# One 512-column matmul for the high and low activations of 256-token stages

## The chip, the core and the metric

The kernel runs on one core of one Trainium2 chip. A core has five engines that run side by side, each with its own in-order instruction queue: TensorE (PE in the profile; its weight loads are shown apart as PEld), VectorE (DVE), ScalarE (ACT), GpSimd (POOL) and SyncE (SP), which here issues DMAs. TensorE multiplies a loaded block of weights (128 x 128) with columns that stream past it and adds the products up in PSUM, which has 8 banks of 512 fp32 values in each of 128 partitions. VectorE and ScalarE read PSUM; everything else lies in SBUF. The metric is the device time of one execution in microseconds.

## The reference, cut to what matters

Three transformer layers run over 256 tokens of width 1024: one hybrid layer (a gated delta rule and a linear recurrent unit, then an MLP), a norm, and two layers of a second kind, before which 16 meta tokens are put in front. All of it is fp32.

```python
# block 1
x = x + mix @ w_out
m = rmsnorm(x, norm_mlp_w)
u = relu(m @ w_ff1)                   # 1024 -> 4096
x = x + (u * u) @ w_ff2
x = rmsnorm(x, final_norm_w)
# block 2: 16 meta tokens in front, then twice
h = h + 0.5 * swiglu(rmsnorm(h), gate, up, down)      # silu(x @ gate) * (x @ up) @ down, 1024 -> 2816
q, k, v, a, b, g_sb, g_conv = split(rmsnorm(h) @ w_in)
y_sb = stick_breaking_attention(q, k, v) @ w_attn_out
y_conv = silu(layernorm(conv31(a * sigmoid(b)))) @ w_conv_out
h = h + (sigmoid(g_sb) * y_sb + sigmoid(g_conv) * y_conv) @ w_out
h = h + 0.5 * swiglu(rmsnorm(h), gate, up, down)
return rmsnorm(h)[:, 16:]
```

## The kernel before

**Layout.** Activations lie transposed: channels in the partitions, tokens in the columns. A stage multiplies weights W, 128 x 128 at a time, with the tokens as the moving columns. A stage has 272 columns while the meta tokens are still needed and 256 where they are not: all of block 1, and of layer 1 of block 2 the queries, both gates, both branch outputs, the output projection and the last swiglu.

**Three products for one.** To come near fp32, every operand is held as a high and a low part in the type fp32r (`h`, `lo` for weights; `x.hi`, `x.lo` for activations, made by `split` and `split_scaled`). One k step, that is 128 input channels for one tile of 128 output channels, is three matmuls into the same bank: high weights by high activations (L532), high weights by low activations (L533), low weights by high activations (L534). Each one has its own weight load.

**The stream of weights.** `plan` lists all tiles of weights in the order of use. The kinds that matter here: `ff1`, `ff2` (block 1's MLP), `gate`, `up`, `down` (swiglu), `q`, `gc`, `gs`, `ys`, `yc`, `o2` (mixer of block 2). A unit is up to 8 k steps of one tile (up to 1024 columns). SyncE brings chunks of two units from HBM into `raw`; ScalarE copies a unit to its high part `wh` (`emit_high`); VectorE, or GpSimd for the units listed in `POOLED`, subtracts to get the low part `wl` (`emit_split`). There are 5 buffers of `wh`, 4 of `wl`, and splits run up to three units (`LEAD`) ahead of TensorE.

**Order by hand.** The program writes the order of every queue when it is built. `job` issues the k steps of one tile and calls `tick` after each. All other work is written as flows (Python generators); a table `clk` holds the expected time of each engine, every helper (`act`, `tt`, `ts`, `stt`, `cp`) moves it by an assumed cost, and `tick` lets a flow go on once its inputs are expected to be there, then lays out weight splits while VectorE's clock is not past TensorE's. A flow that is not told to yield lays its operations directly behind each other. The conv taps of the mixer have the state "F": they fill VectorE where it is free.

**Reading the banks.** After a job a flow reads its bank and gives it back (`give`): `do_ff1` (relu on VectorE, square on ScalarE, split into `hid`), `do_ff2`, `evac` in `swiglu` (scale the gate by `R`, silu on ScalarE, product with the up bank, split into `hid`), `residual` (add to `H`, the input and square sums of the next norm), and in the mixer `keep` (q, v), `rows_mul` (k, a, b and the gates), `do_ys` and `do_yc` (products with the sigmoid gates).

**Places of the activations.** `XS` holds the high parts of all k tiles in one tile and the low parts in another, so the two parts of one k tile lie far apart. The core of a k step is

```python
xh, xl = x.hi(k, o, n), x.lo(k, o, n)
nc.tensor.matmul(acc, h[:, s], xh, start=first and done == 0, stop=False)
nc.tensor.matmul(acc, h[:, s], xl, start=False, stop=False)
nc.tensor.matmul(acc, lo[:, s], xh, start=False, stop=last and done == total - 1)
```

Of the kernel before, what the change touches and what calls it, by code (L numbers as in the profile page):

```python
# [16 lines left out]
T1 = 256  # L17
T2 = T1 + NM
KD = 8
# [16 lines left out]
LIMIT0 = 5.0  # L36
ORDER1 = [(c, t) for c in "kqxgvz" for t in range(4)]

# [68 lines left out]
def layout():  # L107
    """units: (job, k tiles, chunk, first column in the chunk); chunks: (offset, columns)."""
# [37 lines left out]
class Arena:  # L146
    """Scratch of the phases: ranges of one tile, by first fit."""
# [61 lines left out]
class Flow:  # L209
    """A chain of operations that is laid out between the others; t: when its last one is expected to end."""  # L210
# [11 lines left out]
def tile_hybrid_blocks(  # L222
# [173 lines left out]
    def force(cond):  # L396
        """Lays out flows, the earliest first, until cond() holds."""
# [108 lines left out]
    def job(kind, x, n, o=0, bank_=None, last=True, start=None):  # L506
        """The products of one tile of output channels over tokens o to o + n, added to those in a bank, if one
        is given; returns the bank."""
# [8 lines left out]
        acc = bank_[:, 0:n]  # L517
        mine = job_units[j]
        total = sum(len(units[u][1]) for u in mine)
        done = 0  # L520
        for u in mine:
# [4 lines left out]
            for i, k in enumerate(units[u][1]):  # L526
# [5 lines left out]
                nc.tensor.matmul(acc, h[:, s], xh, start=first and done == 0, stop=False)  # L532
                nc.tensor.matmul(acc, h[:, s], xl, start=False, stop=False)  # L533
# [7 lines left out]
    def pair(kinds, x, n, o=0):  # L541
        """Two tiles of output channels side by side, the last k tiles after all others."""
# [20 lines left out]
    def rsqrt(s, n):  # L563
        """s (128 x n, in SBUF, overwritten) to s ** -0.5."""
# [23 lines left out]
    def tok_sums(acc, n):  # L588
        """Sums over the channels, one token per partition, a column per block of tokens."""
# [7 lines left out]
    def to_rows(r, n, out=None):  # L597
        """Columns r, one token per partition, as a row in every partition."""
# [9 lines left out]
    def norm_rows(acc, n, inv, eps, out, src, ev, r=None):  # L608
        """out = rsqrt(inv * sum over the channels + eps) in every partition, once src has come."""
# [14 lines left out]
    def root_norm(accs, n, r):  # L624
        """r = (sum over the channels / 1024 + 1e-6) ** -0.5, one token per partition."""
# [13 lines left out]
    class XS:  # L639
        """A stream input: high and low parts of k tiles of n tokens, in one of the two fixed places or in a pool."""  # L640

        def __init__(self, n, k=KD, pool=None, name=None, place=None, o=0):
            if pool is not None:
                self.place = None
                both = [pool.tile([128, k, n], F32R, name=f"{name}{i}") for i in range(2)]
            else:
                self.place = place or places.pop(0)
                both = [p[:, 0:k * n].rearrange("p (a b) -> p a b", a=k) for p in self.place]
            self.h, self.l = both
# [8 lines left out]

        def done(self):
            if self.place:  # L660
                places.append(self.place)

    places = [
        tuple(const.tile([128, KD * T2], F32R, name=f"x{i}{j}") for j in range(2)) for i in range(2)
    ]
# [21 lines left out]
    # =================== block 1: mixer ===================  # L687
# [58 lines left out]
    def room(*dims):  # L746
        """A block of scratch, once there is one."""
# [195 lines left out]
    def sums(i):  # L943
        """rsqrt of the sums of squares of k (0) or q (1), a column per chunk and head."""
# [44 lines left out]
    def sides(c):  # L989
        """What the recurrence over a chunk takes besides the inverse."""  # L990
# [40 lines left out]
    def chunk(c):  # L1031
        """One chunk of 128 tokens, all heads, up to its output."""
# [42 lines left out]
        # the inverse of the unit triangle, blocks doubling from 2 to 128  # L1075
# [195 lines left out]
    # =================== block 1: output projection, MLP ===================  # L1271
    xb = XS(T1, place=xa.place)
    places.remove(xa.place)
    ev_sq2, ev_r2 = Event(), Event()

    def residual(b, m, x, g, sums, ev, o=0, scale=None, add=tt, free=True, bank=None):
        """H += scale * b; the next norm's input and its sums of squares."""
        hm = H[:, m, o:T2]
        if scale is None:
            tt(hm, hm, b[:, 0:T2 - o], ADD)  # L1280
        else:
            t = yield from slot()
            tt(t[:, 0:T2 - o], b[:, 0:T2 - o], scale, MUL)
# [39 lines left out]
    def do_ff1(b, m):  # L1323
        us = yield from slot()
        u = us[:, 0:T1]
        ts(u, b[:, 0:T1], 0.0, ALU.max)
        give(b)
        act(u, u, AF.Square)
# [26 lines left out]
    def do_ff2(b, m):  # L1355
        t = yield from slot()
        tt(t[:, 0:T1], b[:, 0:T1], R2[:, 0:T1], MUL)
        give(b)
        tt(X(m), X(m), t[:, 0:T1], ADD)
# [46 lines left out]
    # =================== block 2 ===================  # L1406
# [432 lines left out]
```

## Time and profile before

| | us |
|---|---|
| median of 3 runs | 1558.58 |
| lowest and highest run | 1553.17, 1559.71 |
| span of the profiled execution | 1560.1 |
| mean granted TensorE clock of that execution | 0.988 |

| stage (from the span's start, by the chain and the timeline) | us |
|---|---|
| block 1: mixer and output projection | 0 to 182 |
| block 1: ff1 and ff2 (256 columns) | 182 to 366 |
| block 2, layer 0 (272 columns) | 366 to 972 |
| layer 1: first swiglu (272 columns) | 972 to 1171 |
| layer 1: mixer (272 and 256 columns) | 1171 to 1363 |
| layer 1: last swiglu (256 columns) | 1363 to 1550 |
| last norm and output | 1550 to 1560 |

The page names an instruction by its line, engine, operation and tiles (written one, arrow, read ones). Nearly all VectorE and ScalarE work carries the line of a helper (L284 for `tt`, L295 for `stt`, L272 for `act`), so groups are told apart by their tiles. Durations of matmuls are modelled and overlap, each lasting longer than the distance to the next, so what a matmul costs is read from the distance of starts, or from a stretch of time divided by its count of matmuls. A VectorE operation of 256 columns is likewise shown with 0.42 us while the next one may start 0.34 us after it.

### The profile page before, as it was taken

The numbers are of one execution on the slowest core, as the hardware profiler recorded it, in microseconds if no ns is written. First come the engines' busy times: TensorE is split into PE (matmuls) and PEld (weight loads), VectorE is DVE, ScalarE is ACT, GpSimd is POOL, SyncE is SP. The second block draws the span as 40 slices with busy tenths as digits, with TensorE's granted clock in tenths as the row PEclk, the third lists the DMA queues.
The fourth block names the chain that finished last, engine by engine and source line by source line (L and its number), as shares of the span: only waits on it lengthen the run. The fifth ranks groups of instructions, "written<-read, shape, count | busy, mean of one in ns | idle before, by whom it ended". The sixth has DMA issues, their size and how long they took to land.

```text
span 1560.1 us, 29338 instructions
## 1 busy us (share of the span) xinstructions
PE 1528.2 (98%) x12160; PEld 1488.3 (95%) x12160; DVE 1065.3 (68%) x1884; ACT 800.1 (51%) x1351; POOL 164.4 (11%) x146
## 2 busy tenths in 40 slices
PE   7999999999999999999999999999999999999997
PEld 7898999999999999889999999999999989999997
DVE  5887866667555578877765555655558976866654
ACT  4568666544444444545544444444444555555443
POOL 3230300000000011114400000000001113500000
PEclk8999999999999999999999999999999999999999
DMA  6312555554545543323555454554554423555552
GB/s 227 136 55 82 184 187 183 183 184 164 188 163 176 176 162 135 136 86 131 175 178 188 155 174 157 191 187 160 172 183 160 162 84 109 175 204 190 183 174 76
DMA packets 36373, 248.75 MB, mean 159 GB/s; under 512 B 3984, under 2 KB 5264, under 8 KB 12304
## 3 DMA queue, kind: packets, MB, share of 16 engines
q1 hardware_dynamic: 35248, 245.63, 44.5%
q8 instruction: 95, 1.56, 0.4%
q10 hardware_dynamic: 992, 1.26, 0.2%
q14 instruction: 38, 0.31, 0.1%
HBM read 245.82 MB, written 1.05 MB: 158 GB/s over the span
## 4 chain that ended last, share of the span: by engine, by line
PE 90%; DVE 6%; ACT 2%; issue 1%; POOL 0%; DMA 0%; POOLq 0%; DVEq 0%; SPq 0%; ACTq 0%
PE bank L532 28%; PE bank L534 27%; PE bank L533 27%; PE bank L315 6%; DVE arena L295 2%; DVE arena L284 1%; PE bank L319 1%; DVE wl L284 1%; ACT arena L272 1%; DVE H L284 1%; ACT wh L272 1%; DVE x L284 0%; DMA H<-in_xt_dram 0%; POOL acc L307 0%; DVE co L284 0%
## 5 line engine op out<-in xcount | busy, mean ns | idle before, releaser
L532 PE MATMUL bank<-x,wh 128*128 128x272 f32 (+1 forms) x2624 | 766.9, 292 | 11.5 <-ACT x L272 10.6
L534 PE MATMUL bank<-x,wl 128*128 128x272 f32 (+1 forms) x2624 | 756.0, 288 | 3.6 <-DVE wl L284 3.4
L533 PE MATMUL bank<-x,wh 128*128 128x272 f32 (+1 forms) x2624 | 754.7, 288 | 2.3 <-DVE x L284 1.6
L284 DVE TENSOR_TENSOR wl<-raw,wh 128x1024 fp32r<-128x1024 f32 (+4 forms) x453 | 528.5, 1168 | 207.0 <-PE bank L534 168.8
L272 ACT ACTIVATE wh<-raw 128x1024 fp32r<-128x1024 f32 (+4 forms) x510 | 495.6, 977 | 279.6 <-PE bank L533 219.7
L532 PEld LDWEIGHTS bank<-x,wh 128*128 128x128 f32 x2624 | 500.5, 191 | 16.1 <-ACT x L272 11.7
L533 PEld LDWEIGHTS bank<-x,wh 128*128 128x128 f32 x2624 | 503.4, 192 | 5.0 <-DVE x L284 2.9
L534 PEld LDWEIGHTS bank<-x,wl 128*128 128x128 f32 x2624 | 500.1, 191 | 4.7 <-DVE wl L284 4.7
L534 PE MATMUL bank<-hid,wl 128*128 128x272 f32 (+1 forms) x960 | 273.8, 285 | 0.0
L532 PE MATMUL bank<-hid,wh 128*128 128x272 f32 (+1 forms) x960 | 273.6, 285 | 0.0
L533 PE MATMUL bank<-hid,wh 128*128 128x272 f32 (+1 forms) x960 | 273.0, 284 | 0.0
L532 PEld LDWEIGHTS bank<-hid,wh 128*128 128x128 f32 x960 | 180.9, 188 | 0.0
L533 PEld LDWEIGHTS bank<-hid,wh 128*128 128x128 f32 x960 | 180.9, 188 | 0.0
L534 PEld LDWEIGHTS bank<-hid,wl 128*128 128x128 f32 x960 | 180.5, 188 | 0.0
L491 POOL TENSOR_TENSOR wl<-raw,wh 128x512 fp32r<-128x512 f32 (+3 forms) x57 | 106.6, 1884 | 321.4 <-ACT wh L272 171.4
L284 DVE TENSOR_TENSOR tmp<-bank,R 128x272 f32<-128x272 f32 (+1 forms) x184 | 78.8, 430 | 69.2 <-PE bank L534 66.9
L272 ACT ACTIVATE tmp<-tmp 128x272 f32<-128x272 f32 (+1 forms) x140 | 59.3, 425 | 115.4 <-DVE tmp L284 78.5
L295 DVE SCALAR_TENSOR_TENSOR bank<-arena,C,bank 128x272 f32<-128x272 f32 (+1 forms) x232 | 102.0, 492 | 4.9 <-ACT bank L272 3.8
L1482 POOL MEMSET arena<- 128x1 f32 x10 | 0.5, 99 | 779.1 <-PE bank L534 779.1
L315 PE MATMUL bank<-arena 128*128 128x128 f32 (+7 forms) x528 | 77.6, 286 | 1.1 <-ACT arena L272 0.9
L284 DVE TENSOR_TENSOR hid<-tmp,hid 128x272 fp32r<-128x272 f32 (+1 forms) x120 | 51.7, 433 | 38.1 <-ACT hid L272 38.1
L272 ACT ACTIVATE x<-H,C 128x272 fp32r<-128x272 f32 (+2 forms) x64 | 30.0, 486 | 87.7 <-DVE H L284 87.2
(210 smaller groups left out, 1068.4 us busy)
## 6 DMA issues: line engine op xcount, KB each, us to landing
raw<-in_w_dram SPq DMA_DIRECT2D x187, 1024.0 KB, 4.8
raw<-in_w_dram SPq DMA_DIRECT2D x32, 960.0 KB, 4.7
raw<-in_w_dram SPq DMA_DIRECT2D x16, 896.0 KB, 4.6
raw<-in_w_dram SPq DMA_DIRECT2D x2, 512.0 KB, 5.9
H<-in_xt_dram SPq DMA_DIRECT2D x1, 544.0 KB, 6.6
LG<-in_lgw_dram SPq DMA_DIRECT2D x1, 512.0 KB, 6.3
out_dram<-H SPq DMA_DIRECT2D x2, 256.0 KB, 2.2
LM<-in_cm_dram SPq DMA_DIRECT2D x1, 448.0 KB, 5.5
```

Of the source, the lines that this page charges most:

```text
L272: nc.scalar.activation(out, in_, func, scale=scale, **kw)
L284: nc.vector.tensor_tensor(out=out, in0=a, in1=b, op=fn)
L295: nc.vector.scalar_tensor_tensor(out=out, in0=a, scalar=s, in1=b, op0=op0, op1=op1)
L315: nc.tensor.matmul(out, lhsT, rhs, start=start, stop=stop)
L319: nc.tensor.transpose(out, in_, identity)
L491: nc.gpsimd.tensor_tensor(out=lo[:, 0:n], in0=raw[c][:, o:o + n], in1=wh[i][:, 0:n].bitcast(F32), op=SUB)
L532: nc.tensor.matmul(acc, h[:, s], xh, start=first and done == 0, stop=False)
L533: nc.tensor.matmul(acc, h[:, s], xl, start=False, stop=False)
L534: nc.tensor.matmul(acc, lo[:, s], xh, start=False, stop=last and done == total - 1)
L1482: nc.gpsimd.memset(a.f[:, w:w + 1], 1.0)
```

## The change

For the kinds in a new list, and only where a stage has 256 columns, the high and the low part of a k tile are put side by side, and one matmul streams both past the high weights: 512 columns, into the two halves of the bank. The low weights still meet the high part alone, in the first half. The bank then holds two sums that have to be added when it is read.

```diff
+WIDE = ("ff1", "ff2", "q", "gc", "gs", "ys", "yc", "o2", "gate", "up", "down")
...
+        wide = kind in WIDE and n == 256
+        both = bank_[:, 0:2 * n].rearrange("p (a b) -> p a b", a=2) if wide else None
...
-                nc.tensor.matmul(acc, h[:, s], xh, start=first and done == 0, stop=False)
-                nc.tensor.matmul(acc, h[:, s], xl, start=False, stop=False)
+                if wide:
+                    nc.tensor.matmul(both, h[:, s], x.pair(k, o, n), start=first and done == 0, stop=False)
+                else:
+                    nc.tensor.matmul(acc, h[:, s], xh, start=first and done == 0, stop=False)
+                    nc.tensor.matmul(acc, h[:, s], xl, start=False, stop=False)
                 nc.tensor.matmul(acc, lo[:, s], xh, start=False, stop=last and done == total - 1)
...
+    def whole(out, b, n):
+        cp(out, b[:, n:2 * n])
+        tt(out, out, b[:, 0:n], ADD)
```

`XS` becomes one tile with the parts of a k tile next to each other; the sizes stay the same. The planner's expected cost of a k step stays as it was.

```diff
-                both = [pool.tile([128, k, n], F32R, name=f"{name}{i}") for i in range(2)]
+                self.both = pool.tile([128, k, 2, n], F32R, name=name)
...
+            self.h, self.l = self.both[:, :, 0], self.both[:, :, 1]
...
+        def pair(self, k, o, n):
+            return self.both[:, k, :, o:o + n]
```

Every reader of such a bank changes. `whole` is a ScalarE copy of the second half and a VectorE addition of the first.

```diff
 # residual: H += scale * b
             tt(hm, hm, b[:, 0:T2 - o], ADD)
+            if wide:
+                tt(hm, hm, b[:, 256:512], ADD)
...
+            if wide:
+                whole(t[:, 0:256], b, 256)
+                tt(t[:, 0:256], t[:, 0:256], scale, MUL)
 # do_ff1
-        ts(u, b[:, 0:T1], 0.0, ALU.max)
+        whole(u, b, T1)
         give(b)
-        act(u, u, AF.Square)
+        stt(u, u, 0.0, u, ALU.max, MUL)
 # do_ff2
-        tt(t[:, 0:T1], b[:, 0:T1], R2[:, 0:T1], MUL)
+        whole(t[:, 0:T1], b, T1)
         give(b)
+        tt(t[:, 0:T1], t[:, 0:T1], R2[:, 0:T1], MUL)
 # swiglu, evac, where n == 256
+                whole(g, ga, n)
+                give(ga)
+                tt(g, g, R[:, 0:n], MUL)
             act(g, g, AF.Silu)
+                whole(h, ua, n)
+                give(ua)
             yield "V"
+                tt(h, g, h, MUL)
 # mixer: rows_mul where oo > 0, keep for the queries, and
+        def gated(g, b):
+            if n == 256:
+                t = yield from slot()
+                whole(t[:, 0:n], b, n)
+                give(b)
+                tt(g, g, t[:, 0:n], MUL)
+                free_tmps.append(t)
```

In `rows_mul` the sum of the halves is followed by the multiplication with `R`, in SBUF; in `keep` the sum takes the place of a copy; `do_ys` and `do_yc` use `gated`. All other lines of the diff take out comments and docstrings.

More of the change, by code (lines that the diff above doesn't have):

```diff
@@ L657, in lo @@
             return self.l[:, k, o:o + n if n else self.n]
+        def pair(self, k, o, n):
+            return self.both[:, k, :, o:o + n]
         def done(self):
-            if self.place:
+            if self.place is not None:
                 places.append(self.place)
-    places = [
-        tuple(const.tile([128, KD * T2], F32R, name=f"x{i}{j}") for j in range(2)) for i in range(2)
-    ]
+    places = [const.tile([128, 2 * KD * T2], F32R, name=f"x{i}") for i in range(2)]
     def X(k):
@@ L1272, in tile_hybrid_blocks, with residual @@
     xb = XS(T1, place=xa.place)
-    places.remove(xa.place)
+    places.pop()
     ev_sq2, ev_r2 = Event(), Event()
-    def residual(b, m, x, g, sums, ev, o=0, scale=None, add=tt, free=True, bank=None):
+    def residual(b, m, x, g, sums, ev, o=0, scale=None, add=tt, free=True, bank=None, wide=False):
         hm = H[:, m, o:T2]
@@ L1422, in evac @@
             g, h = gs[:, 0:n], hs_[:, 0:n]
-            tt(g, ga[:, 0:n], R[:, 0:n], MUL)
-            give(ga)
+            if n == 256:
+                whole(g, ga, n)
+                give(ga)
+                tt(g, g, R[:, 0:n], MUL)
+            else:
+                tt(g, ga[:, 0:n], R[:, 0:n], MUL)
+                give(ga)
             act(g, g, AF.Silu)
+            if n == 256:
+                whole(h, ua, n)
+                give(ua)
             yield "V"
-            tt(h, g, ua[:, 0:n], MUL)
-            give(ua)
+            if n == 256:
+                tt(h, g, h, MUL)
+            else:
+                tt(h, g, ua[:, 0:n], MUL)
+                give(ua)
             free_tmps.append(gs)
@@ L1451, in swiglu @@
             start_flow(
-                residual(b, m, nx, None if final else next_g(m), acc1[:, 0:n], ev_sq, o, R5[:, 0:n])
+                residual(b, m, nx, None if final else next_g(m), acc1[:, 0:n], ev_sq, o, R5[:, 0:n],
+                         wide=n == 256)
             )
@@ L1488, in rows_mul @@
             yield from wait(ev_r)
-            tt(out, b[:, 0:T2 - oo], R[:, oo:T2], MUL)
-            give(b)
+            if oo:
+                whole(out, b, 256)
+                give(b)
+                tt(out, out, R[:, oo:T2], MUL)
+            else:
+                tt(out, b[:, 0:T2 - oo], R[:, oo:T2], MUL)
+                give(b)
             if ev is not None:
@@ L1494, in keep @@
         def keep(out, b, ev):
-            cp(out, b[:, 0:out.shape[-1]])
+            if out.shape[-1] == 256:
+                whole(out, b, 256)
+            else:
+                cp(out, b[:, 0:out.shape[-1]])
             give(b)
@@ L1683, in mixer @@
         x.done()
+        def gated(g, b):
+            if n == 256:
+                t = yield from slot()
+                whole(t[:, 0:n], b, n)
+                give(b)
+                tt(g, g, t[:, 0:n], MUL)
+                free_tmps.append(t)
+            else:
+                tt(g, g, b[:, 0:n], MUL)
+                give(b)
         def do_ys(b, m):
             yield from wait(ev_gates[8 + m])
-            tt(SG.f[:, m], SG.f[:, m], b[:, 0:n], MUL)
-            give(b)
+            yield from gated(SG.f[:, m], b)
             note(ev_ys[m])
@@ L1692, in do_yc @@
             yield from wait(ev_gates[m], ev_ys[m])
-            tt(SC.f[:, m], SC.f[:, m], b[:, 0:n], MUL)
-            give(b)
+            yield from gated(SC.f[:, m], b)
             tt(SC.f[:, m], SC.f[:, m], SG.f[:, m], ADD)
@@ L1710, in mixer @@
             b = pairs["o2"].pop(0) if m < 2 and "o2" in PAIRED else job("o2", mo, n)
-            start_flow(residual(b, m, nx, next_g(m), acc1[:, 0:n], ev_sq, o, add=pt))
+            start_flow(residual(b, m, nx, next_g(m), acc1[:, 0:n], ev_sq, o, add=pt, wide=n == 256))
         mo.done()
```

6 lines of the change are left out of this document (3 added, 3 removed).

## The prediction

> **What bounds the kernel now.** I read the page's busy times and its chain first, then the busy times by stage.
>
> ```profile
> span 1560.1 us, 29338 instructions
> PE 1528.2 (98%) x12160; PEld 1488.3 (95%) x12160; DVE 1065.3 (68%) x1884; ACT 800.1 (51%) x1351; POOL 164.4 (11%) x146
> ...
> PE 90%; DVE 6%; ACT 2%; issue 1%; POOL 0%; DMA 0%; POOLq 0%; DVEq 0%; SPq 0%; ACTq 0%
> ```
>
> TensorE is 90% of the chain that ended last. So the stages have to be read for what one matmul costs there. The windows view gives, for each stretch, its length, then PE, weight loads (PEld), DVE, ACT and POOL, each with a count, then the granted clock, the DMA share and GB/s. The stretches are ff1, ff2, a 272-token gate/up, and the last gate/up with 256 tokens.
>
> ```profile
> 205.00:265.00 60.00, 60.00 (x512) 60.00 (x511) 40.55 (x65) 38.25 (x65) 0.00 (x0) 1.00 0.53 188
> 280.00:360.00 80.00, 80.00 (x679) 80.00 (x678) 48.72 (x75) 37.18 (x54) 0.00 (x0) 1.00 0.49 172
> 380.00:480.00 100.00, 100.00 (x795) 100.00 (x794) 62.72 (x90) 48.82 (x68) 0.00 (x0) 1.00 0.51 179
> 1375.00:1475.00 100.00, 100.00 (x851) 100.00 (x850) 63.01 (x89) 50.98 (x72) 0.00 (x0) 1.00 0.55 193
> ```
>
> No stretch has a hole in PE, and the clock is full. A 256-column matmul costs 60/512 to 80/679 = 117 to 118 ns, one of 272 columns 100/795 = 126 ns. A k step is three of them: 353 ns at 256 columns. Is that the columns, or something else? The timeline of the decay products has TensorE load 128 columns of the same 4-byte weights but stream only 8 or 16 columns:
>
> ```profile
> 22.52 2.63 PE L315 MATMUL bank<-wb,x 128*128 128x16 f32 x23
> ```
>
> The view was cut at 25.00, so 23 starts lie within 2.48 us: at most 113 ns apart with hardly a column to stream. **That is the price of a weight load**, and the 256-column matmuls at 117.5 stand just above it. What do columns alone cost? The layer norm's fp32 products show it, at 256 and at 272 columns, each with the row that follows it:
>
> ```profile
> 1294.52 1.89 PE L315 MATMUL bank<-arena,mean 128*128 128x256 f32 x8
> 1296.06 0.47 PE L532 MATMUL bank<-x,wh 128*128 128x256 f32 x1
> ```
>
> ```profile
> 700.33 2.00 PE L315 MATMUL bank<-arena,mean 128*128 128x272 f32 x8
> 701.96 0.49 PE L532 MATMUL bank<-x,wh 128*128 128x272 f32 x1
> ```
>
> Eight instructions start within 1.54 us, so they are at most 1.54/7 = 220 ns apart, and 1.63/7 = 233 with 272 columns. The 16 extra columns cost 13 ns, 0.8 ns each. Weight matmuls can take no more than 117.5/256 = 0.46 ns a column, so an fp32 instruction passes its columns twice, at 0.4 ns. An instruction with one load and 512 column passes therefore takes at most 220 ns: the load is out of sight behind the columns. This is the nearest thing in the trace to the new matmul.
>
> **The change, part by part.** *Matmuls removed.* The forms view counts the k steps with 256 columns:
>
> ```profile
> L532 PE MATMUL bank<-x,wh 128*128 128x256 f32 x1088 | 317.2, 292 | 8.3 <-ACT x L272 7.4 <-ACT arena L272 0.9
> ...
> L532 PE MATMUL bank<-hid,wh 128*128 128x256 f32 x432 | 121.4, 281 | 0.0
> ...
> L532 PE MATMUL bank<-co,wh 128*128 128x256 f32 x32 | 9.1, 283 | 0.0
> L532 PE MATMUL bank<-ys,wh 128*128 128x256 f32 x32 | 9.0, 283 | 0.0
> ```
>
> Of the 1088, 24 tiles of 8 k steps in block 1's mixer and 16 of 4 in its output projection are not in WIDE: 832 remain. With 432 + 64 that is 1328 k steps: ff1 256, ff2 256, last gate/up 352, last down 176, layer 1's mixer 288. Each gives up one matmul and one load, and no column. The new step is one 512-column matmul (215 ns: a little under the bound of 220, as the 1.54 us also hold the eighth start) and one 256-column one, at today's 117.5 because the next load still sits behind its columns: 333 ns, 20 less than 353. A floor comes from a quiet stretch:
>
> ```profile
> 48.87 0.28 PE L532 MATMUL bank<-x,wh 128*128 128x256 f32 x1
> ...
> 49.21 0.28 PE L532 MATMUL bank<-x,wh 128*128 128x256 f32 x1
> ```
>
> Three matmuls in 0.34 us are 113 ns each; with that the step is 328 and gives 25. The other end is a 512-column matmul at twice 117.5: nothing saved. I take 20, nearest to the layer norm rows. For the 1040 feed-forward steps that is **-20.9 us**.
>
> The Trainium skill speaks against it: "TensorE: Matmul & The Clock Gate", section Back-to-back issue gap, gives N/2.4 + 2.5 ns for an isolated matmul, so a removed one would return 2.5 ns, an estimated 3.3 us for all 1328. The trace disagrees at 256 columns: 109 by that rule, 117.5 in the rows.
>
> *Reading the bank, ff1.* Every evacuation gains a ScalarE copy of one half and a VectorE add; ff1's max and ScalarE square become one VectorE operation. The timeline of one tile before, by engine:
>
> ```profile
> 232.06 0.42 DVE L289 TENSOR_SCALAR tmp<-bank 128x256 f32<-128x256 f32 x1 [0.94 <-PE bank L534]
> 232.40 1.22 DVE L284 TENSOR_TENSOR wl<-raw,wh 128x1024 fp32r<-128x1024 f32 x1
> 233.54 0.42 DVE L284 TENSOR_TENSOR hid<-tmp,hid 128x256 fp32r<-128x256 f32 x1
> ```
>
> ```profile
> 232.97 0.42 ACT L272 ACTIVATE hid<-tmp 128x256 fp32r<-128x256 f32 x1
> 233.30 1.05 ACT L272 ACTIVATE wh<-raw 128x1024 fp32r<-128x1024 f32 x1
> ```
>
> ```profile
> 1549.72 0.42 DVE L284 TENSOR_TENSOR tmp<-bank,R 128x256 f32<-128x256 f32 x1 [6.01 <-PE bank L534]
> 1550.18 0.42 DVE L284 TENSOR_TENSOR H<-H,tmp 128x256 f32<-128x256 f32 x1
> ```
>
> VectorE goes on 0.34 us after a 256-column operation, 0.46 if the next needs its result, 1.14 after a weight split. New ff1 tile: add 0.46 + max-square 0.46 + split 1.14 + low part 0.34 = 2.40 us, where TensorE needs 8 x 0.333 = 2.67. It fits, with 0.27 us for the wait on the copy. Cost 0.
>
> *Gate/up* is narrower:
>
> ```profile
> 1453.39 1.23 DVE L284 TENSOR_TENSOR wl<-raw,wh 128x1024 fp32r<-128x1024 f32 x1 [1.14 <-PE bank L534]
> 1454.53 0.42 DVE L284 TENSOR_TENSOR tmp<-bank,R 128x256 f32<-128x256 f32 x1
> 1455.43 0.42 DVE L284 TENSOR_TENSOR tmp<-tmp,bank 128x256 f32<-128x256 f32 x1 [0.49 <-ACT tmp L272]
> 1456.34 0.42 DVE L284 TENSOR_TENSOR hid<-tmp,hid 128x256 fp32r<-128x256 f32 x1 [0.48 <-ACT hid L272]
> ```
>
> ```profile
> L272 ACT ACTIVATE arena<-bank 128x256 f32<-128x256 f32 x12 | 4.4, 368 | 2.7 <-PE bank L534 2.7
> ```
>
> Two splits 2.28; add, scale, add, product 4 x 0.46 = 1.84; low part 0.34; and an open wait of about 0.8, because the second bank's copy (0.37) is laid behind the silu (0.42) and VectorE's add right behind it: 5.26 us against 16 x 0.333 = 5.33. What stands behind that add on VectorE is the next weight split, and TensorE waits for that; three units of lead cover one late split, not one in every tile. If the 0.48 wait on the hidden copy also stays open, 5.74 exceeds today's 5.65. Bounds: 0 to 352 x 20 ns = 7.1 us lost. I take **+1.5**.
>
> *ff2, down, o2, q, gc, gs* get 0.46 to 0.9 us of VectorE per tile of 2.7 to 10.7 us: hidden. q, gc and gs share VectorE with the filler conv taps, which give way. *ys and yc* (4 k steps a tile) are another matter:
>
> ```profile
> L284 DVE TENSOR_TENSOR arena<-arena 128x256 f32<-128x256 f32 x7 | 5.9, 848 | 0.2
> L284 DVE TENSOR_TENSOR x<-arena,x 128x256 fp32r<-128x256 f32 x6 | 4.1, 689 | 0.5 <-ACT x L272 0.5
> L284 DVE TENSOR_TENSOR arena<-arena,bank 128x256 f32<-128x256 f32 x7 | 2.9, 411 | 1.0 <-PE bank L534 1.0
> ```
>
> ```profile
> 1320.93 10.79 POOL L491 TENSOR_TENSOR wl<-raw,wh 128x512 fp32r<-128x512 f32 x8
> ```
>
> ```profile
> 1270.00:1302.00 32.00, 32.00 (x222) 28.02 (x223) 23.57 (x46) 16.44 (x39) 4.76 (x2) 0.95 0.29 102
> 1325.00:1339.00 14.00, 12.73 (x102) 12.13 (x102) 13.14 (x22) 6.52 (x14) 8.55 (x6) 1.00 0.44 154
> ```
>
> From 1270 to 1302, among the gate tiles, VectorE still has 8 of 32 us free. From 1325 to 1339, in yc, it is busy 13.1 of 14 us and PE has holes. While POOL splits weights, VectorE operations with both inputs in SBUF take 0.85, those with one in the bank 0.41. The old product read the bank; the new one reads two SBUF tiles, behind an added bank read. That is 8 x (0.34 to 0.85) = 2.7 to 6.8 us for yc, as much again for ys at worst: I take **+4.5**, which the mixer's other 224 steps (224 x 20 ns) return: net 0, between -5 and +9. The Trainium skill's "GPSIMD Engine Reference", section 8, Key points, states the same contention for VectorE instructions with two SBUF inputs.
>
> *Waits and tails.* The wide matmul needs both halves of x. Where a stage starts, the low part comes one VectorE operation (0.46) behind the high one, so the first matmul moves there; the low-part matmul waited anyway: 0. At the end, copy 0.37 and add 0.46 go in ahead of the scaling at 1549.72: **+0.9**.
>
> Sum: -20.9 + 1.5 + 0 + 0.9 = -18.5 us. The profiled span of 1560.1 lies 1.5 above the median 1558.58 and about at the longest run, so nothing is added around it: 1541.6 for that execution, **1540** for the median. With the bounds, 1530 to 1550.
>
> **Rivals.**
> 1. *The excess goes with the columns:* the 15 ns above 0.4 ns x 256 are a stream slowed in proportion, as 126 ns at 272 columns, 17 above, allows. Then 512 columns take 235, nothing is saved, and +0.9 and +4.5 are left: 1564. Against it: the layer norm's 220. The Trainium skill's gap formula above would end close by, at an estimated 1561. Chance 0.10.
> 2. *VectorE takes gate/up and the mixer's end:* the pace stays 5.65 a tile, the mixer costs 8: 1558.6 - 688 x 20 ns + 0.9 + 8 = 1554. For it: 5.26 of 5.33. Chance 0.14.
> 3. *Slower: the copy out of the bank sits behind a weight copy.* ScalarE runs in order; the weight copy (1.05) waits for TensorE to free a buffer. If VectorE's add waits for it in every tile, gate/up takes 5.26 + 1.05 = 6.3 (22 x 0.66 = +14.5), ff1 2.40 + 1.05 = 3.45 against 2.83 (32 x 0.62 = +20); ff2 and down give 8.7 back, the mixer and tail cost 5.4: 1590. It decides from 2.83 us a tile in ff1, 5.65 in gate/up. Against it: ScalarE is busy 51 of 100 us there. Chance 0.10.
>
> **How the numbers follow.** Forecast 0.66. About 0.5% (7.8 us) is what a measurement of this kernel can tell from no change, so 1550.8 is the line. Faster: the forecast but for its edge, 0.64. Same: that edge 0.02, rivals 1 and 2: 0.26 in all, rounding included. Slower: rival 3, 0.10. The range takes the forecast and rival 2, from 1530 to 1556; rivals 1 and 3, 0.20, are left out.
>
> **What would show it.** In ff2 and down, 8 matmuls in 4 x 333 ns: right; 353: rival 1. Gate/up at 5.3 us a tile: right; 5.65: rival 2; 6: rival 3, with VectorE waiting on ScalarE's bank copies. ys and yc: a longer hole before o2. Wrong altogether if a wide matmul costs over 235 ns, or if the new order delays the conv beyond yc.

## The result and the profile after

| kernel | median us | runs, lowest to highest | span of the profiled execution |
|---|---|---|---|
| before | 1558.22 | 1553.17 to 1559.71 | 1560.1 |
| changed | 1594.4 | 1593.58 to 1599.39 | 1597.6 |

The ratio is 1.0245 (95%: 1.0219 to 1.0271): the changed kernel is slower. This is the line of busy times on its page:

```profile
PE 1528.4 (96%) x10832; PEld 1419.5 (89%) x10832; DVE 1125.0 (70%) x2020; ACT 823.0 (52%) x1443; POOL 162.8 (10%) x146
```

TensorE has 1328 matmuls fewer and is busy for as long as before: 1528.4 against 1528.2 us. So nothing was won on TensorE, and some 37 us of holes came in. First the matmuls. The windows view of the changed kernel, over the same ff1, ff2 and 272-column stretches as before (columns as there):

```profile
205.00:265.00 60.00, 60.00 (x342) 52.08 (x341) 49.10 (x86) 37.42 (x65) 0.00 (x0) 1.00 0.56 191
280.00:360.00 80.00, 80.00 (x454) 69.44 (x453) 51.01 (x89) 39.91 (x68) 0.00 (x0) 1.00 0.52 178
380.00:480.00 100.00, 100.00 (x804) 100.00 (x803) 64.67 (x96) 50.12 (x70) 0.00 (x0) 1.00 0.53 179
```

In ff1's 60 us, 342 matmuls at two to a k step are as many steps as the 512 matmuls before at three to a step. The first and the last start of one line's matmuls give the pace more sharply. These are, in ff1, the wide matmul of the changed kernel and then the first matmul of a step before:

```profile
L536 PE MATMUL bank<-x,wh x171: 397/397/398, 204.9 to 265.0; 128*128 128x512 f32 x171
```

```profile
L532 PE MATMUL bank<-x,wh x170: 281/281/281, 205.0 to 264.7; 128*128 128x256 f32 x170
```

60.1/170 = 353.5 ns a step now, 59.7/169 = 353.3 before. By the distances of starts the new step is 235 + 118 ns. The weight loads do have room now (PEld 52 of 60 us), but the step is no shorter for it. The third window is a stage that the diff leaves at three matmuls, and it went from 795 to 804 of them: something in the change makes 272-column stages about 1% faster.

Then the holes, by the first matmul of each stage in the timelines of the two profiled executions:

| from, to | before us | after us | difference |
|---|---|---|---|
| start to the first ff2 matmul | 268.6 | 269.9 | +1.3 |
| ff2 | 90.9 | 90.4 | -0.4 |
| 272-column stages, up to the first query tile | 836.3 | 830.2 | -6.1 |
| layer 1's queries, values, gates, up to ys | 115.3 | 113.9 | -1.4 |
| ys to the first yc matmul | 12.4 | 41.8 | **+29.4** |
| yc to the first o2 matmul | 11.5 | 16.1 | +4.5 |
| o2 and the last gate/up | 152.0 | 160.5 | +8.5 |
| down and the end | 73.1 | 74.8 | +1.7 |

Most of the loss sits between ys and yc. There, after the last ys matmul, the timeline of PE in the changed kernel holds these pieces (later steps of the norm and of yc are left out):

```profile
1330.28 1.22 PE L316 MATMUL bank<-arena,mean 128*128 128x256 f32 x2 [11.27 <-DVE arena L296]
1334.35 1.22 PE L316 MATMUL bank<-arena,mean 128*128 128x256 f32 x2 [2.85 <-DVE arena L296]
1337.42 2.02 PE L316 MATMUL bank<-ones,tmp 128*128 128x1 f32 x8 [1.84 <-DVE tmp L285]
1346.30 0.79 PE L536 MATMUL bank<-co,wh 128*128 128x512 f32 x1 [3.29 <-DVE co L285]
```

The layer norm's first products wait 11.27 and 2.85 us for VectorE's L296, which writes `arena`: the conv taps. Behind them the norm runs alone, each step waiting for the one before. When yc starts, from 1346 to 1350 us, the granted clock is 0.50 (it was 1.00 in yc before), so part of yc's own +4.5 us goes with that clock. Where were the taps? The windows view for that line alone (L295 before, L296 after) gives VectorE's busy time and count in five stretches: the tiles up to the gates, two stretches of gate tiles, ys, and the hole, which only the changed kernel has. Before:

```profile
1180.00:1220.00 40.00, 19.18 (x45) 1.00 0.43 154
1220.00:1265.00 45.00, 23.90 (x57) 1.00 0.40 141
1265.00:1295.00 30.00, 7.86 (x18) 0.94 0.29 102
1295.00:1316.00 21.00, 0.49 (x3) 1.00 0.26 91
```

After:

```profile
1180.00:1220.00 40.00, 14.52 (x34) 1.00 0.41 135
1220.00:1265.00 45.00, 16.80 (x40) 1.00 0.40 138
1265.00:1295.00 30.00, 0.97 (x2) 1.00 0.31 106
1295.00:1316.00 21.00, 2.61 (x6) 1.00 0.31 101
1316.00:1336.00 20.00, 14.74 (x35) 0.71 0.31 106
```

Some 35 of 120 taps moved out of the gate tiles to where nothing else is left to do. It was not for want of time on VectorE. This is the third of these windows for all engines, after:

```profile
1265.00:1295.00 30.00, 28.78 (x155) 21.09 (x154) 18.31 (x29) 16.36 (x40) 4.58 (x2) 1.00 0.31 106
```

VectorE is busy 18.3 of 30 us there; before the change it was 22.3. The taps were laid too late in its queue, whose order is fixed when the program is built.

### The profile page after: what moved, and what is told of

Read it like the earlier page. It is cut to its first block, busy times and chain, and to the rows that moved or that the text cites. A ratio compares the mean times of both kernels' runs of the same rounds, so it can differ in the third digit from the quotient of the medians.

```text
span 1597.6 us, 26831 instructions
## 1 busy us (share of the span) xinstructions
PE 1528.4 (96%) x10832; PEld 1419.5 (89%) x10832; DVE 1125.0 (70%) x2020; ACT 823.0 (52%) x1443; POOL 162.8 (10%) x146
## 5 line engine op out<-in xcount | busy, mean ns | idle before, releaser
L538 PE MATMUL bank<-x,wh 128*128 128x272 f32 (+1 forms) x1792 | 525.4, 293 | 10.8 <-ACT x L273 9.9
L539 PE MATMUL bank<-x,wh 128*128 128x272 f32 (+1 forms) x1792 | 516.6, 288 | 1.5 <-DVE x L285 0.8
L538 PEld LDWEIGHTS bank<-x,wh 128*128 128x128 f32 x1792 | 341.4, 191 | 14.3 <-ACT x L273 10.7
L539 PEld LDWEIGHTS bank<-x,wh 128*128 128x128 f32 x1792 | 342.7, 191 | 3.6 <-DVE x L285 1.7
L536 PE MATMUL bank<-x,wh 128*128 128x512 f32 x832 | 303.3, 406 | 5.9 <-DVE x L285 2.9
L536 PEld LDWEIGHTS bank<-x,wh 128*128 128x128 f32 x832 | 159.6, 192 | 45.9 <-issue 4.4
L285 DVE TENSOR_TENSOR tmp<-tmp,bank 128x256 f32<-128x256 f32 (+1 forms) x190 | 80.9, 426 | 116.5 <-ACT tmp L273 115.9
L536 PE MATMUL bank<-hid,wh 128*128 128x512 f32 x432 | 152.7, 397 | 0.0
L539 PE MATMUL bank<-hid,wh 128*128 128x272 f32 x528 | 152.6, 289 | 0.0
L538 PE MATMUL bank<-hid,wh 128*128 128x272 f32 x528 | 151.4, 287 | 0.0
L296 DVE SCALAR_TENSOR_TENSOR bank<-arena,C,bank 128x272 f32<-128x272 f32 (+1 forms) x232 | 102.3, 492 | 6.4 <-ACT bank L273 5.1
L538 PEld LDWEIGHTS bank<-hid,wh 128*128 128x128 f32 x528 | 99.6, 189 | 0.0
L539 PEld LDWEIGHTS bank<-hid,wh 128*128 128x128 f32 x528 | 99.5, 188 | 0.0
L536 PEld LDWEIGHTS bank<-hid,wh 128*128 128x128 f32 x432 | 81.1, 188 | 20.1
L273 ACT ACTIVATE hid<-tmp 128x272 fp32r<-128x272 f32 (+1 forms) x120 | 51.0, 426 | 86.7 <-DVE tmp L285 51.8
```

The source lines that it names most:

```text
L273: nc.scalar.activation(out, in_, func, scale=scale, **kw)
L285: nc.vector.tensor_tensor(out=out, in0=a, in1=b, op=fn)
L296: nc.vector.scalar_tensor_tensor(out=out, in0=a, scalar=s, in1=b, op0=op0, op1=op1)
L536: nc.tensor.matmul(both, h[:, s], x.pair(k, o, n), start=first and done == 0, stop=False)
```

## The experiments

**Theory.** `whole` puts the ScalarE copy and the VectorE addition directly behind each other. The expected clock of VectorE is thereby moved to the end of the copy, wait and all; a tap may go only while that clock is at most 0.5 us ahead of TensorE's, so the waits push the taps out. **Rivals:** the 512-column matmuls or the feed-forward reads cost the time; or the added work on VectorE has no room. A second question is TensorE's: why does a 512-column matmul take 235 ns?

**1. The layout alone**, `WIDE` empty; **2. feed-forward wide, 3. mixer wide, 4. the changed kernel with a yield in the read.**

```diff
-WIDE = ("ff1", "ff2", "q", "gc", "gs", "ys", "yc", "o2", "gate", "up", "down")
+WIDE = ()                                               # e1
+WIDE = ("ff1", "ff2", "gate", "up", "down")             # e2
+WIDE = ("q", "gc", "gs", "ys", "yc", "o2")              # e3
 # e4: WIDE as in the change, and all callers "yield from whole(...)"
     def whole(out, b, n):
         cp(out, b[:, n:2 * n])
+        yield "V"
         tt(out, out, b[:, 0:n], ADD)
```

> Only the new layout of the activations (high and low part of a k tile side by side), no wide matmul, every bank read as before. In the changed kernel the 272-column stages, which have no wide matmul, ran from 360.4 to 1190.6 us, 6.1 us shorter than before. If the layout does that: 1552, and a 272-column matmul at 125 ns instead of 126. If that was chance or came from the other order of the work: 1558. Both theories of the loss (columns: a column costs 0.46 ns whatever the load; order: the taps of the mixer's convolution are laid out too late) expect no slowdown here.

> Wide matmuls and added reads in the feed-forward stages alone (1040 k steps), the mixer as before. Columns theory: 353 ns a k step as before, the reads are hidden, so the layout run plus 1 to 3 us. Load theory of the prediction (a 512-column matmul hides its load and takes 215 ns): 20 us less than the layout run. If VectorE cannot keep up in gate/up: the layout run plus 8 or more, with gate/up at over 5.65 us a tile.

> Wide matmuls and added reads in layer 1's mixer alone (288 k steps), feed-forward stages as before. If the whole loss is the mixer's (late taps, then the knock-on in o2 and the first tiles of gate/up): the layout run plus 38 to 44 us, with some 30 us between the first ys and the first yc matmul more than before. If the feed-forward reads share in it: the layout run plus 25 to 30.

> The changed kernel with one difference: between the copy and the addition of a bank's halves the flow yields, so that convolution taps and weight splits can be laid out in between; the same instructions, in another order. Order theory: the taps go back into VectorE's idle time (3 to 4 us in each 10 us from 1265 to 1305), the 29 us hole between ys and yc mostly closes: 1560 to 1568. Capacity theory (VectorE has no time for the added reads): within 5 us of the changed kernel, 1590 to 1598.

Each ratio is against the kernel before as it was timed beside that run, whose median lay between 1558 and 1563 us. The last two columns are from the profiled executions, in us.

| kernel | median us | ratio to before, 95% | ys to yc | yc to o2 |
|---|---|---|---|---|
| before | | 1 | 12.4 | 11.5 |
| changed | 1594.4 | 1.0245 (1.0219 to 1.0271) | 41.8 | 16.1 |
| e1_layout_alone | 1552.95 | 0.9935 (0.9913 to 0.9957) | 12.4 | 11.5 |
| e2_ff_wide | 1552.61 | 0.9927 (0.9899 to 0.9955) | 12.4 | 11.5 |
| e3_mixer_wide | 1591.65 | 1.0172 (1.0142 to 1.0201) | 42.6 | 15.8 |
| e4_yield_in_read | 1567.87 | 1.0042 (1.0029 to 1.0055) | 19.8 | 18.2 |

Wide matmuls in the feed-forward stages change nothing that the medians can tell (2 against 1): 1040 of the 1328 steps give no time back. In the last gate/up of e2_ff_wide, the wide matmuls

```profile
L536 PE MATMUL bank<-x,wh x267: 397/397/398, 1375.8 to 1469.8; 128*128 128x512 f32 x134
```

start every 94.0/266 = 353.4 ns: VectorE's added reads fit. The stages by themselves show one thing more. These are ff1 with the layout alone, and the last gate/up of e3_mixer_wide, both with three narrow matmuls to a step:

```profile
205.00:265.00 60.00, 60.00 (x531) 60.00 (x530) 42.22 (x69) 39.50 (x67) 0.00 (x0) 1.00 0.55 194
```

```profile
1400.00:1460.00 60.00, 60.00 (x532) 60.00 (x531) 40.59 (x59) 32.97 (x47) 0.00 (x0) 1.00 0.62 214
```

Here a 256-column matmul starts every 60/531 = 113 ns and a step takes 340 ns, 13 less than before and 13 less than the wide step. In the last gate/up of e1_layout_alone the same narrow steps took 353 again (512 matmuls in 60 us). What decides between the two paces stays open; where the narrow step has the faster one, the wide step loses against it, an estimated 3 us in ff1 (some 230 steps had the faster pace there).

Most of the loss is the mixer's: 3 stands 0.0237 above the layout alone, the change 0.0310. The other 0.007, some 11 us, shows only where both parts are wide. In the profiled executions 7.9 us of it lie in o2 and the last gate/up, 152.6 us in 3 and 160.5 in the change, and an estimated 4 us of these are gate/up's narrow steps in 3 (some 320 of the 352 at 340 ns instead of 353).

A yield, which changes neither a matmul nor an operation, takes back 0.020 of the 0.0245, some 32 us (4): **the order of the work**, not its amount. It lets weight splits as well as taps go in between, so that it does not yet price the taps alone. The new layout alone, with each queue's instructions in the same order as before, is faster than before by 0.65%.

**6 to 8. The order by other levers, and the rest.** 6 leaves the gates at three matmuls; 7 raises the taps' threshold; 8 is the yield with ys and yc at three matmuls. A later run, **10**, leaves every instruction of the reads as it is and only does not book the wait for q, k, the gates, ys and yc:

```diff
-WIDE = ("ff1", "ff2", "q", "gc", "gs", "ys", "yc", "o2", "gate", "up", "down")
+WIDE = ("ff1", "ff2", "q", "ys", "yc", "o2", "gate", "up", "down")        # e6
+WIDE = ("ff1", "ff2", "q", "gc", "gs", "o2", "gate", "up", "down")        # e8, on e4
-FILL = 0.5
+FILL = 2.0                                                                # e7
 # e10
-    def whole(out, b, n):
+    def whole(out, b, n, book=True):
+        f = cur[0]
+        t, eng = f.t, f.eng
         cp(out, b[:, n:2 * n])
+        if not book:
+            f.t, f.eng = t, eng
         tt(out, out, b[:, 0:n], ADD)
```

> The changed kernel with the two gates (gc, gs) left as three 256-column matmuls and read as before. Order theory (the wait in each two-step read of a gate is booked on VectorE's expected clock, so the conv taps are laid out too late): the gates are 16 of the tiles read while the taps should go, so most taps return to the gate tiles, the gap between ys and yc falls from 42 to 12 to 25 us, and the time to 1565 to 1580. Rival (the late taps come from ys and yc themselves, or VectorE is truly short of time): the gap stays near 42 and the time near 1592.

> The changed kernel with one number altered: the conv taps are laid out while VectorE's expected clock is at most 2.0 us, not 0.5 us, ahead of TensorE's. No matmul and no reading of a bank differs. Order theory: the taps are no longer held back by the waits booked in the reads, the gap between ys and yc falls from 42 to 12 to 22 us, the time to 1562 to 1575. Rival (VectorE has no room for the taps before yc, since the reads take it): the gap stays above 35, or it shrinks and TensorE loses as much before ys; time 1585 to 1600.

> The kernel with the yield between copy and addition (e4_yield_in_read) with ys and yc left as three 256-column matmuls and read as before. Theory of the rest: of the 15 us by which e4_yield_in_read is behind e1_layout_alone, those between the start of ys and the start of o2 (38 us there, 24 in e1_layout_alone) come from the two-step reads in ys and yc, so they go: 1554 to 1560. Rival: they come from the gates' later reads and the taps that they push; then ys to o2 still takes 33 us or more and the time stays at 1564 to 1570.

> The changed kernel with the same instructions and the same two-step reads; only the planner's clock differs: for q, k, gates, ys and yc the addition is booked on VectorE by its own cost, without the wait for ScalarE's copy. Order theory: what delays the taps is the booked wait, not VectorE's work, so the laid order has the taps done within the gate tiles, the gap between ys and yc falls from 42 to 12 to 22 us, and the time to 1562 to 1578, near e4_yield_in_read. Rival: the wait itself costs VectorE the time, so that taps laid earlier only push reads and weight splits later: the holes move into the gate tiles (ys starts at 1315 or later instead of 1304) and the time stays above 1585.

| kernel | median us | ratio to before, 95% | ys to yc | yc to o2 |
|---|---|---|---|---|
| e6_gates_narrow | 1575.32 | 1.0090 (1.0060 to 1.0121) | 17.5 | 19.5 |
| e7_fill_2us | 1600.03 | 1.0253 (1.0218 to 1.0289) | 37.8 | 15.8 |
| e8_yield_ysyc_narrow | 1559.73 | 0.9981 (0.9962 to 1.0001) | 16.7 | 13.2 |
| e10_wait_not_booked | 1577.93 | 1.0136 (1.0108 to 1.0164) | 27.3 | 13.0 |

The gates are where the taps were held back (6): with them narrow 0.0155 of the 0.0245 is gone. **The threshold was a miss (7):** the gap fell by 4 us only and the time not at all. (The threshold also rules the filler convolutions of block 1, which muddies the run: in 7 the first ff2 matmul starts at 277.0 us, 7 us later than in the changed kernel.) The program's own clocks, written out while it lays its queues, say why. Over the 128 k steps of the 16 gate tiles:

```
kernel   VectorE's expected lead   ScalarE's    k steps at which a tap   taps laid
         over TensorE, mean us     lead, mean   may go (lead <= limit)   there
before   1.06                      1.07         47 (0.5 us)              53
changed  1.87                      2.17         20 (0.5 us)              25
e4       0.92                      1.26         48 (0.5 us)              55
e7       3.32                      3.55         23 (2.0 us)              27
e10      0.78                      0.91         50 (0.5 us)              55
```

The second column is VectorE's expected time less TensorE's. In the plan the copy goes to the end of ScalarE's queue, behind the attention's work; the addition follows it, and VectorE's clock jumps to ScalarE's. What comes next on ScalarE starts from there: the two leads pull each other up. A higher limit lets the lead grow with it. Not booking the wait (10) brings the lead down and the 55 taps back, which is worth 0.011 of the 0.0245, some 17 us. The windows view of the tap's line, as above, shows them in the gate tiles on the chip too (60 in these two stretches, 75 before, 42 in the changed kernel):

```profile
1220.00:1265.00 45.00, 16.16 (x37) 1.00 0.33 115
1265.00:1295.00 30.00, 9.98 (x23) 1.00 0.40 132
```

The layer norm's products now start without a wait, but 10's gap came out at 27.3, over the 12 to 22 expected. The timelines of PE, DVE and ScalarE in e10_wait_not_booked show the new hole, with what each waits for in brackets:

```profile
1326.43 0.77 PE L536 MATMUL bank<-co,wh 128*128 128x512 f32 x1 [8.87 <-DVE co L285]
```

```profile
1324.57 0.42 DVE L285 TENSOR_TENSOR tmp<-tmp,bank 128x256 f32<-128x256 f32 x1 [3.72 <-ACT tmp L273]
1325.03 0.92 DVE L285 TENSOR_TENSOR arena<-arena,tmp 128x256 f32<-128x256 f32 x1
1325.87 1.42 DVE L285 TENSOR_TENSOR co<-arena,co 128x256 fp32r<-128x256 f32 x4
```

```profile
1323.33 0.42 ACT L273 ACTIVATE co<-arena 128x256 fp32r<-128x256 f32 x1
1323.65 0.61 ACT L273 ACTIVATE wh<-raw 128x512 fp32r<-128x512 f32 x1
1324.17 0.36 ACT L273 ACTIVATE tmp<-bank 128x256 f32<-128x256 f32 x1
```

The last ys bank's copy stands on ScalarE behind the four silus and a weight copy; VectorE's addition waits 3.72 us for it, and behind the addition stand the low parts of `co`, for which TensorE waits 8.87. That wait is real, booked or not. In 10 o2 and the last gate/up also take 162.3 us, against 156.7 in 4. With the yield instead (4) PE still has two holes there, in its timeline:

```profile
1311.39 0.58 PE L540 MATMUL bank<-ys,wl 128*128 128x256 f32 x1 [4.25 <-DVE wl L285]
...
1322.30 0.77 PE L536 MATMUL bank<-co,wh 128*128 128x512 f32 x1 [4.43 <-DVE co L285]
```

Leaving ys and yc narrow takes them down to 2.07 and 0.73 us and the time from 1.0042 to 0.9981 (8), some 9 us; ys to o2 falls from 38.0 to 29.9. What is left of 8 over 2, 0.5%, comes with wide q, gates and o2 and with the yield in the other reads; it was not taken apart.

**5, 9 and 11: what a wide matmul costs.** Blocks of matmuls were put ahead of the last norm, so these kernels' own times say nothing of the change. These are two pieces of the added code, cut: the first block of e5_probe, 512 columns, and a wide k step of e9_kstep_probe:

```diff
+    for i in range(N_):
+        nc.tensor.matmul(pbk[0][:, 0:512], w8(i), PA[:, 0:512], start=i == 0, stop=i == N_ - 1)
...
+            nc.tensor.matmul(both, hw(k), PV[:, k], start=i == 0, stop=False)
+            nc.tensor.matmul(wide_bank[:, 0:256], lw(k), PV[:, k, 0], start=False, stop=i == n - 1)
```

> The changed kernel with a block of matmuls added ahead of the last norm, alone on the chip's core: 32 each of fp32r with 512, 256, 128 and 384 columns and of bf16 with 512 and 256 columns, 8 plain fp32 with 512 columns, and then 96 fp32r of 512 columns during which VectorE and ScalarE each do 40 operations of 256 columns. Columns theory (a column of fp32r costs 0.46 ns, whatever the matmul's width, and the weight load lies beside it): at full clock 235 ns for 512 columns, 176 for 384, 118 for 256, and 128 columns near 113 or below; the same with the other engines busy. Load theory, that of the prediction: 215 for 512, 161 for 384, 113 to 118 for 256, 113 for 128. A third reading, that other engines' work slows the columns: 512 columns take 215 to 220 while VectorE and ScalarE are idle and 235 in the last stretch while they are busy. For bf16 there is no row so far: if its 512 columns take 215, the 0.46 belongs to the type fp32r; if 235, to any type.

> The changed kernel with blocks of k steps of the two forms added ahead of the last norm: wide (one fp32r matmul of 512 columns, one of 256) and slim (three of 256), first with TensorE alone, the last slim block there with the low part 4 k tiles away from the high one; then with ScalarE copying and VectorE subtracting 1024 columns each; then with 1 MB weight transfers arriving; then with both. In the earlier probe TensorE alone took 227 ns for 512 columns and 120 for 256, so alone a wide step should take 347 and a slim one 360, while both take 353 in the kernel. Which of its surroundings makes them equal? If transfers into SBUF slow the long stream: wide rises to 353 or more with transfers, and slim stays at 353 to 360. If the other engines' reads do it: wide rises to 353 beside the copies and subtractions, and with transfers alone stays at 347. If it is in the alternation of 512 and 256 columns itself: wide takes 353 alone as well, and slim, which alternates between two activations and two weight blocks, takes 353 and not 360. The low part far away should cost the slim step 0 by the rows so far, or up to 3 ns by the 272-column stages, which became 1 ns a matmul faster with the new layout.

> The changed kernel with nine blocks of 32 k steps ahead of the last norm, TensorE alone: 512 columns as one run of addresses; 512 columns as two halves, as the change writes them; 512 flat and then 256; the two halves 2048 columns apart and then 256; the wide step and the slim step with high and low weights in tiles of their own; slim steps of 272 columns with the low part next to the high one and 4 k tiles away; and 256 by high weights, 256 by low weights. So far 512 columns repeated took 227 ns, 235 in alternation with 256. If the two-halves form is what costs 8 ns: the second block takes 235, the first and the third 227. If the alternation of widths is: the first two take 227, the third 235. If the weights lying in one tile with others matter: the slim step goes from 360 to 353. If the place of the low part is what made the 272-column stages 1 ns a matmul faster: 272 next to each other takes 1 ns less than apart; if both are equal, that gain has another cause.

These are single lines of e5_probe, with the duration (durations overlap) and the first and the last start, which are rounded to 0.1 us, so that a distance worked out from 32 of them is good to 3 ns: fp32r (shown as f32) with 512, 256 and 128 columns, bf16 with 512 and 256.

```profile
L1790 PE MATMUL bank<-x,x x32: 387/389/401, 1584.0 to 1591.0; 128*128 128x512 f32 x32
L1792 PE MATMUL bank<-x,x x32: 278/283/283, 1591.3 to 1595.0; 128*128 128x256 f32 x32
L1794 PE MATMUL bank<-x,x x32: 224/274/280, 1595.1 to 1598.5; 128*128 128x128 f32 x32
L1798 PE MATMUL bank<-pb,identb x32: 379/379/391, 1604.2 to 1610.9; 128*128 128x512 bf16 x32
L1800 PE MATMUL bank<-pb,identb x32: 272/273/273, 1611.1 to 1614.5; 128*128 128x256 bf16 x32
```

Last less first start over 31 gives 226, 119, 110, 216 and 110 ns; by the single starts it is a steady 227, 120, 111, 216 and 109. Neither theory was exact: when one width repeats, an fp32r matmul costs 11 ns more than a bf16 one at both widths, and 256 more columns cost 107 ns in either type. (The bf16 blocks use one weight block, the fp32r blocks eight in turn; this probe does not tell the type from the weights.) With 128 columns a matmul takes 111 ns, only 9 less than with 256, so that the columns alone do not set it; it is close to the 113 that the prediction read as the price of a load. The layer norm's fp32 products, 215 ns for twice 256 columns in the prediction, go at bf16's rate: in the same probe a record of 512 columns of fp32 takes 429 ns, twice 215.

Then comes the k step. This is the wide matmul of e9_kstep_probe, first with TensorE alone, then beside transfers, copies and subtractions:

```profile
L1795 PE MATMUL bank<-x,x x32: 387/398/403, 1602.2 to 1613.1; 128*128 128x512 f32 x32
L1795 PE MATMUL bank<-x,x x36: 395/398/486, 1674.5 to 1687.0; 128*128 128x512 f32 x36
```

10.9/31 = 352 and 12.5/35 = 357 ns, the second with a wait of 90 ns in its first step; after it both go on at 353. The single starts alternate about 235 and 118 in both, and also with transfers alone or engines alone. The narrow step of three (called slim in the expectation) took 360 in all. The windows view shows what ran beside the second:

```profile
1675.50:1687.00 11.50, 11.50 (x67) 9.96 (x67) 11.19 (x10) 11.15 (x12) 0.00 (x0) 1.00 1.02 422
```

So it is none of the surroundings. In e11_forms_probe TensorE is alone. Its lines are, in order: 512 columns flat; 512 in two halves; 512 flat, each followed by a 256; the two halves far apart, each followed by a 256; the wide and the narrow step with weights in tiles of their own; steps of 272 columns with the low part next to the high one; the same with the low part apart.

```profile
L1793 PE MATMUL bank<-x,x x32: 387/389/401, 1580.9 to 1588.0; 128*128 128x512 f32 x32
L1796 PE MATMUL bank<-x,x x32: 389/389/389, 1588.2 to 1595.3; 128*128 128x512 f32 x32
L1799 PE MATMUL bank<-x,x x32: 389/398/403, 1595.5 to 1606.4; 128*128 128x512 f32 x32
L1804 PE MATMUL bank<-x,x x32: 395/398/403, 1606.8 to 1617.8; 128*128 128x512 f32 x32
L1809 PE MATMUL bank<-x,wh x32: 388/397/398, 1618.1 to 1629.0; 128*128 128x512 f32 x32
L1813 PE MATMUL bank<-x,wh x32: 280/281/281, 1629.4 to 1640.3; 128*128 128x256 f32 x32
L1818 PE MATMUL bank<-x,wh x32: 283/288/291, 1640.7 to 1652.3; 128*128 128x272 f32 x32
L1823 PE MATMUL bank<-x,wh x32: 283/288/291, 1652.7 to 1664.3; 128*128 128x272 f32 x32
```

Repeated, 512 columns take 229 ns (227 once steady) in either form; as soon as a 256 follows, the step takes 352 to 355 (353 to 354 by the single starts), flat, halved or far apart. The kernel's two steps side by side, fifth and sixth line, both take 10.9/31 = 352 ns (353 by the single starts): the kernel's result, reproduced with nothing else running. The alternation of widths turns 227 into 235; what in TensorE does so stays open. The narrow step took 360 in e9_kstep_probe, where all weights lay in one tile, and 353 here; the wide step took 353 in both. The last two lines are equal, so with TensorE alone the nearness of the low part does not make the 272-column steps faster; what did stays open too.

## Why the prediction was wrong

It said 1540, within 1530 to 1556; 1594.4 came. Point by point:

1. **The 512-column matmul at 215 ns: the failed step of the gain.** "The new step is one 512-column matmul (215 ns...) and one 256-column one": 333 predicted, 353.5 measured; the -20.9 us of the feed-forward and the 4.5 us that the mixer was to return came out as 0. The layer norm's fp32 products were called the nearest thing in the trace, but they are another type: 512 columns of bf16, or 256 of fp32 twice, take 215 to 216 ns, 512 of fp32r 227 repeated and 235 in a k step. (The eight rows there are records, two to each of four fp32 instructions: the 8 of e5_probe left 16. The 215 ns of a record are not touched by this.) Rival 1 had the number, 235, and a sign of it was in the rows: 126 ns at 272 columns is 0.5 ns for each of the 16 more, not 0.4. Its reason, a stream slowed in proportion, is not what the runs show: 256 more columns cost 107 ns in e5_probe, 0.42 ns each, and 256 columns went at 113 ns in ff1 of e1_layout_alone. Its 235 was right in part by luck.
2. **Conv taps "which give way": the failed step of the loss.** q, gc and gs were priced at VectorE's busy time and called hidden, since 8 of 32 us were free. VectorE was still free afterwards (18.3 of 30 us busy). But a tap goes by the plan's clock, in which a read that waits counts as work. The order cost some 32 us in all (4), of which some 17 come back when only the booked wait is left out (10); the prediction had put nothing there. Its last sentence named the sign, a conv delayed beyond yc, and gave it no price and no chance.
3. **ys and yc at +4.5: right mechanism, too small.** Two-step reads there cost some 9 us (8 against 4). The reason shows in the changed kernel's timeline in ys: while GpSimd split weights, first line, the product with two inputs in SBUF took 1.28 us, and 0.43 when GpSimd was idle:

```profile
1310.44 1.29 POOL L492 TENSOR_TENSOR wl<-raw,wh 128x512 fp32r<-128x512 f32 x1 [0.61 <-DVE wl L285]
```

```profile
1310.74 1.28 DVE L285 TENSOR_TENSOR arena<-arena,tmp 128x256 f32<-128x256 f32 x1
...
1315.61 0.43 DVE L285 TENSOR_TENSOR arena<-arena,tmp 128x256 f32<-128x256 f32 x1
```

   The larger part, holes behind weight splits and `co` that queue behind a read, was not in the sum.
4. **ff1 at 0: right.** VectorE went from 40.55 to 49.10 of 60 us and PE shows no hole. **Gate/up at +1.5**: nothing is to be seen, 353.4 ns a step; with the old pace of 5.65 us a tile, 5.26 us of VectorE had more room than the sum gave it. **The tail at +0.9**: down and the end took 1.7 us more.
5. **The layout at nothing, unsaid: wrong** by 0.65%, some 10 us (1): a term that the sum did not have.
6. **Rival 3** ended at 1590, close to the result, but that is luck: in ff1 and gate/up no bank copy held up a tile. Its mechanism, a copy behind other work in ScalarE's queue, did act, in the mixer: in the plan's clock of the gates, and for real ahead of yc (10).
7. **o2 and the last gate/up, +8.5**: not foreseen. The layout alone has +4.0 there (156.0 us), so not all of it is the wide matmuls'. The windows view of the changed kernel has 8 us of PE holes and a lower granted clock, 0.77, at its start:

```profile
1362.00:1384.00 22.00, 13.85 (x51) 11.03 (x52) 16.84 (x28) 10.89 (x21) 7.80 (x5) 0.77 0.43 145
```

The Trainium skill's rule in "TensorE: Matmul & The Clock Gate", section Back-to-back issue gap, N/2.4 + 2.5 ns for an isolated matmul at full clock, gives 109 and 216 for 256 and 512 columns. The bf16 lines agree with both; the fp32r ones do not, at 113 to 120 and 227 to 235. A removed matmul did not return 2.5 ns here: the step with three before and the one with two take the same, and ff1's step with three on the new layout takes 13 ns less.

The version that beats both kernels is the layout alone, 0.9935 (0.9913 to 0.9957); wide matmuls in the feed-forward stages add nothing to it that these runs can tell.

## What to carry to other kernels

Before counting on fewer, wider matmuls, find the price of the wide one in its own type and in its own alternation; a block of 32 steps at a kernel's end gave it to the nanosecond. Lay the operands as the kernel has them: the narrow step took 360, 353 or 340 ns by run and place. Where queues are ordered at build time, price a new two-engine step by what it does to the plan's clocks as well: an operation laid directly behind another engine's makes its own engine look busy while it waits, and filler work goes elsewhere. Free time on an engine is cover only if something will be laid into it.

## What the runs showed of the hardware

- fp32r costs 11 ns more per matmul than bf16 when one width repeats (227 against 216, 120 against 109 in e5_probe), and a 512 followed by a 256 takes 235; transfers at 422 GB/s, copies and subtractions beside it change that by nothing.
- Three fp32r matmuls of 256 columns, each with its own load, have two steady paces at a granted clock of 1.00: 113 ns apart (e1_layout_alone in ff1, e3_mixer_wide in gate/up) and 118 (e1_layout_alone in gate/up, the kernel before). What picks one is open.
- After a hole the wide step costs nearly double, at a granted clock of 0.50. In e4_yield_in_read's windows view and PE timeline, behind the 4.43 us hole, from 1323.08 to 1323.72 = 0.64 us:

```profile
1322.00:1325.00 3.00, 2.70 (x9) 2.35 (x10) 0.82 (x3) 0.56 (x2) 0.21 (x1) 0.50 0.82 257
```

```profile
1323.08 0.63 PE L536 MATMUL bank<-co,wh 128*128 128x512 f32 x1
1323.50 0.41 PE L540 MATMUL bank<-co,wl 128*128 128x256 f32 x1
1323.72 0.63 PE L536 MATMUL bank<-co,wh 128*128 128x512 f32 x1
```

- High and low parts of all k tiles in one tile instead of two, with the same queues, gave 0.65%. In the profiled executions 7.0 us of it lie in the 272-column stages between block 2's first matmul and layer 1's mixer, and 5.4 ahead of ff2, where ff1's step went from 353 to 340 ns; o2 and the last gate/up gave 4.0 back. With TensorE alone the place of the low part made no difference to 272-column steps (374 ns both).
